# Opening of a two-layer encoder kernel: parameter loads on another queue, weight blocks cut the other way, gate products between q and k, a shift vector summed into columns

## The chip, the cores and the metric

One Trainium2 chip, one of its cores. The metric is device time in microseconds (us) of one launch. TensorE is called PE below, VectorE DVE, ScalarE ACT, GpSimd POOL and SyncE SP, as in the profile. SP computes nothing here: it issues the weight transfers, one after the other.

## The reference

A trunk of two layers on 256 tokens of width 1024. What matters here of each layer:

```
mod = silu(c) @ w_ada[l] + b_ada[l]                  # 6 vectors of 1024
shift1, scale1, gate1, shift2, scale2, gate2 = split(mod, 6)
h = rms_norm(x, norm1_g) * (1 + scale1) + shift1
mq, mk, mv, mo, mgates, aq, ak, av, gm, ga = split(h @ w_in + b_in)
y_m = mlstm_mixer(mq, mk, mv, mo, mgates, conv_w, ...)   # q, k: convolution over 5 tokens, silu
y_a = bidirectional_gqa(aq, ak, av, ...)                 # 8 heads, 2 key heads, rotary
merged = sigmoid(gm) * (y_m @ w_branch_m) + sigmoid(ga) * (y_a @ w_branch_a)
x = x + gate1 * (merged @ w_out)
h2 = rms_norm(x, norm2_g) * (1 + scale2) + shift2
x = x + gate2 * hierarchical_moe(h2, ...)                # 32 experts, 2 a token, 6 MB of weights each
```

All weights are float32 and are read from memory once. `w_ada` is 25 MB a layer, `w_in` 20 MB, the experts 201 MB.

## The kernel before

Each layer has a mixer (`mixer`) and an expert stage (`experts`).

**Weights** come in transfers of 1 MB into a ring of slots: an arena of 16 slots in SBUF, of which four (0, 1, 2, 15) are always ring slots, and three tiles `B`. Other arena slots join when their contents are dead (`release`, the word `free` in `MIX`) and leave again (`withhold`, the word `hold`: the three tiles go). `plan` is the list of all transfers in order. `pump` issues the next ones as long as a slot that suits is free, and `done` gives a slot back. SP keeps the order of the list, so a transfer that waits for its slot holds up all behind it. Each queue's DMAs take eight semaphores in turn, so that one issue also waits for the landing of the one eight before it.

**Products of the mixer.** `h` lies as channels by tokens, 8 blocks of 128 channels, split into a high and a low part (`hh`, `hl`) of the type that PE multiplies fast; each weight block is split in the same way. A *step* is half of the channels (four blocks, `kh`) against 256 columns of `w_in`: 24 matmuls of 128x256. Its preparation (`prep`) is a cast on ACT (128x1024) and two subtractions (`low`), one on DVE and one on POOL, into one of two buffers `R`. A layer has 38 such steps, in the order of `ORDER`: q, k, akv, aq, v, o, gm, ga (`keys`). A transfer of `w_in` holds all channels of 256 columns and so serves two steps. A finished pair of q or k goes through `fin_qk`: per 128 columns a copy on ACT, one `tensor_scalar` and four `scalar_tensor_tensor` on DVE (the convolution), a silu on ACT. A pair of gm or ga is copied by ACT alone (`fin_g`).

**MIX** is a string per layer, written by hand, which interleaves the steps (numbers) with all other work: the mLSTM's gates (`gates`, `gates2`) and its decay vectors (`dec0` to `dec4`; `dec1` is 12 narrow matmuls that need `lf` from DVE), its heads (`ms`, `mo`), attention (`kr`, `qr`, `as`, `at`, `ao`), and the products with `w_ada` (`r4` to `r11` of this layer, `c0` to `c3` of the next). PE and SP keep the order of the program; a scheduler orders ACT, DVE and POOL.

**Products with `w_ada`.** A block of 512 columns takes two transfers and eight matmuls (`ada_part`, 16 rows of the trace), which leave sums in four rows. ACT and DVE split them, two matmuls with a matrix of ones add them up over the rows (`ada_sum`, rows named `prow`), and the result is either turned into columns (`ada_col`: multiply by the identity and reduce) or added to a vector that is the same in all partitions (`ada_row`).

**Opening of layer 0** (`setup`, then the first part of `mixer`): SP issues two blocks of `w_ada` (4 MB), then all small parameters (`params`, 12 DMAs), then two more blocks, then `w_in`. PE takes block 0, then 1, then the transposed `x` (`pxt`), then 2 and 3; shift1 is in blocks 0 and 1, scale1 in 2 and 3. When all 16 columns of `c1` are there, `hh` and `hl` are made, and the steps begin.

**After the steps**, `dense(4)` runs the first four of eight merge products, then 16 matmuls of one row (`psh`, `psj`) turn shift2 (`sh2b`, a row vector in SBUF) into two sets of columns, for the router (`shT`) and for the experts (`sh2c`). The rest of the merges, the product with `w_out`, the router and the experts follow.

Of the kernel before, what the change touches and what calls it, by code (L numbers as in the profile page):

```python
# [18 lines left out]
P = 128  # L19
# [24 lines left out]
ORDER = (("q", 2), ("k", 2), ("akv", 1), ("aq", 2), ("v", 2), ("o", 2), ("gm", 4), ("ga", 4))  # L44
# [3 lines left out]
    "1 gates 3 gates2 dec0 tables 3 dec1 1 c0 dec2 2 dec3 r5 1 dec4 2 kr 1 qr:0 r11 1 kt 2 qr:1 1 r7 1 hold qt:0 1 ms:0 1 c1 qt:1 2 ms:1 1 as:0 r8 mo:0 mo:1 2 r9 ms:3 1 ms:2 at:0 at:4 r4 as:1 mo:2 1 r10 1 at:1 mo:3 ao:0 at:5 r6 1 ao:2 as:2 mn c2 free:7:13:14 2 mt at:2 1 as:3 2 at:3 c3 at:6 at:7 ao:1 1 ao:3 2",  # L48
    "1 tables 1 gates 2 gates2 dec0 3 dec1 1 dec2 2 dec3 1 dec4 1 kr 2 kt r10 1 qr:0 2 qr:1 r6 1 hold 3 ms:0 qt:1 2 r8 ms:1 1 qt:0 mo:0 as:0 1 r9 mo:1 as:1 1 ms:2 r11 at:0 at:4 ms:3 mo:2 2 at:5 1 at:1 mo:3 ao:0 r7 ao:2 1 as:2 mn free:7:13:14 2 at:2 at:6 1 mt as:3 2 at:3 at:7 ao:1 1 ao:3 2")
# [4 lines left out]
def trunk(ctx, tc, x, c, w_ada, b_ada, norm1_g, w_in, b_in, conv_w, conv_b, mlstm_norm_g, q_norm_g, k_norm_g,  # L54
# [135 lines left out]

    keys = [(nm, j) for nm, n in ORDER for j in range(n)]

# [3 lines left out]
    def stream(l):  # L196

        n = sent = 0
        for w in MIX[l].split():
            if w.isdigit():  # L200
                n += int(w)
            elif is_ada(w) and (w[0] != "c" or l + 1 < depth):
                m = min((n + 1) // 2 + 1, len(keys))
                yield from keys[sent:m]
                sent = max(sent, m)
                yield "c" if w[0] == "c" else "r", int(w[1:])
        yield from keys[sent:]

    g1b, gt2b = at(3, 0, D), at(3, D, D)
    A2b, sh2b = at(4, 0, D), at(4, D, D)  # L210
# [11 lines left out]
    def late_loads2(l):  # L222
        for t, o in ((g1b, 2), (sh2b, 3), (A2b, 4), (gt2b, 5))[l > 0:]:
# [4 lines left out]
    def first_params():  # L228
        first["p"] = params(0, nc.sync)

    for l in range(depth):
        if l == 0:
            for b in range(2):
                plan_ada(0, b)
            add(("params", 0), first_params, None)
            for b in range(2, 4):
                plan_ada(0, b)
        else:
            plan_ada(l, EARLY[0])
        for it in stream(l):  # L240
            if it[0] in DENSE:
                o = DENSE[it[0]] + 256 * it[1]
                add((it[0], l, it[1]), w_in[l].rearrange("(k p) c -> p k c", p=P)[:, :, o:o + 256], (8, 256))
# [13 lines left out]
        for j in range(4):  # L257
            add(("wo", l, j), w_out[l].rearrange("(k p) c -> p k c", p=P)[:, :, 256 * j:256 * j + 256], (8, 256))
# [35 lines left out]
    def params(l, q):  # L294
# [23 lines left out]
        p["gqk"] = gqk  # L318
        return p
# [8 lines left out]
    def setup():  # L328
# [3 lines left out]
        pump()  # L332
        V.memset(condp, 0.0)
# [56 lines left out]
    def ada_part(l, b):  # L390
        pb = ps.tile([P, 512], F32, tag="f", name="pada")
        for h in range(2):
# [4 lines left out]
            done("ada", l, b, h)  # L397
        ph, pw = parts_at[0][:, 0, :], parts_at[0][:, 1, :]
# [10 lines left out]
    def ada_col(l, b, parts):  # L409
# [3 lines left out]
        n = 4 if l == 0 else 2  # L413
        dg = at(5, 0, n, P) if l == 0 else at(8, 1556, n, P)
# [5 lines left out]
    def ada_row(l, b, parts):  # L420
# [3 lines left out]
        dst = {2: g1b, 3: sh2b, 4: A2b, 5: gt2b}[kind][:, hs]  # L424
# [7 lines left out]
    def mixer(l, p):  # L432
# [3 lines left out]
        parts_at[:] = [pool.tile([P, 2, 512], F32R, name="part")]  # L436
        st["phase"] = 4 * l
# [14 lines left out]
        def prep():  # L452
# [65 lines left out]
        def fin_qk(j, pq):  # L518
            pre = rot("pre", 5, 0, 2, S + 4)
# [939 lines left out]
```

## Time and profile before

| | us |
|---|---|
| median of three runs | 1512.65 |
| their range | 1510.78 to 1512.72 |
| the profiled execution | 1509.83 |
| its span, first to last instruction | 1508.0 |

PE is busy for 1357.6 us, 90% of the span, DVE for 650.1 us, ACT for 396.5 us, POOL for 266.5 us. 519.77 MB are read. The span falls into four stages: mixer 0 to about 312 us, experts 0 to about 770 us, mixer 1 to about 1036 us, experts 1 to the end. In the page's 40 slices the transfers move about 420 GB/s in both expert stages and between 204 and 346 GB/s in the mixers. A busy share says which engine to look at; what ends a wait is read from the rows of the stage. Idle time of an engine stands in brackets behind the instruction that came after it, with what ended it.

### The profile page before, as it was taken

To read this page: it belongs to the slowest core of one execution; us is meant where nothing else is said; L and a number is where in the kernel's file an instruction comes from. 1 tells how busy PE (TensorE), PEld (TensorE's weight loads), DVE (VectorE), ACT (ScalarE), POOL (GpSimd) and SP (SyncE) were. 2 spreads that over 40 slices of the span, in tenths; PEclk is the share of its full clock that TensorE was granted. 3 is DMA by queue.
4 is the path that set the end of the run, shared out by engine and by line. 5 is a ranking of instruction groups with operands and counts; after the bars stand their busy time and mean duration, and the time that the engine had idled before them with its cause. 6 is when DMAs were issued, how large, how long until landed. Compare 5 with 4: busy or idle time off the path is not lost. (4 is left out here: it accounts for less than half of the span.)

```text
span 1508.0 us, 20315 instructions
## 1 busy us (share of the span) xinstructions
PE 1357.6 (90%) x7878; PEld 794.2 (53%) x7879; DVE 650.1 (43%) x1404; ACT 396.5 (26%) x729; POOL 266.5 (18%) x306
## 2 busy tenths in 40 slices
PE   5799999969999989879978999997999999888996
PEld 1678779934434434334338888994434443334432
DVE  2697774633232322223258867554223323213223
ACT  1444664421111111011035366633111111101101
POOL 1545334500000000000015543560000000000000
PEclk8889999989999999999989999998999999999998
DMA  8967697769999999999996666766999999999995
GB/s 293 338 204 257 226 346 270 273 268 420 422 421 421 420 421 422 421 419 376 418 375 227 217 216 238 241 251 231 421 422 420 421 421 420 421 421 419 376 421 216
DMA packets 146698, 522.24 MB, mean 346 GB/s; under 512 B 15660, under 2 KB 62962, under 8 KB 98466
## 3 DMA queue, kind: packets, MB, share of 16 engines
q1 hardware_dynamic: 140898, 517.20, 87.4%
q10 hardware_dynamic: 4880, 1.87, 0.5%
q0 software_dynamic: 816, 1.78, 0.5%
q8 instruction: 65, 1.06, 0.3%
q14 instruction: 39, 0.32, 0.1%
HBM read 519.77 MB, written 1.05 MB: 345 GB/s over the span
## 5 line engine op out<-in xcount | busy, mean ns | idle before, releaser
L1213 PE MATMUL pgu<-arena 128*64 128x512 f32 x1456 | 349.7, 594 | 20.2 <-DMA arena<-in_w_up_dram 11.7
L1213 PEld LDWEIGHTS pgu<-arena 128*64 128x64 f32 x1456 | 115.1, 137 | 223.5 <-issue 172.7
L1222 DVE SCALAR_TENSOR_TENSOR arena<-pgu,wsl,arena 128x512 f32<-128x512 f32 x32 | 36.4, 1137 | 383.4 <-PE pgu L1213 383.4
L1238 PE MATMUL pd<-arena 128*64 128x512 f32 x720 | 177.7, 594 | 7.3 <-ACT arena L1229 7.3
L441 POOL TENSOR_TENSOR R<-arena,R 128x512 fp32r<-128x512 f32 (+1 forms) x86 | 125.9, 1466 | 168.3 <-ACT R L459 109.9
L1169 POOL TENSOR_TENSOR arena<-oh,arena 128x256 f32<-128x256 f32 x32 | 19.5, 615 | 741.6 <-DVE oh L1163 470.0
L494 PE MATMUL pd<-R,R 128*128 128x256 f32 x1008 | 136.9, 294 | 8.2 <-ACT R L641 5.1
L509 PE MATMUL pd<-R,R 128*128 128x256 f32 x1056 | 134.9, 285 | 4.8 <-DVE R L441 4.8
L494 PEld LDWEIGHTS pd<-R,R 128*128 128x128 f32 x1008 | 129.4, 199 | 18.0 <-issue 6.9
L509 PEld LDWEIGHTS pd<-R,R 128*128 128x128 f32 x1056 | 128.8, 191 | 10.4 <-DVE R L441 5.4
L1249 DVE TENSOR_TENSOR y<-pd,arena 128x512 f32<-128x512 f32 x64 | 44.1, 691 | 202.7 <-PE pd L1238 167.3
L1213 PE MATMUL pgu<-B,arena 128*64 128x512 f32 x432 | 118.1, 594 | 2.7 <-DMA B<-in_w_up_dram 2.7
L441 DVE TENSOR_TENSOR R<-arena,R 128x512 fp32r<-128x512 f32 (+1 forms) x102 | 83.8, 827 | 58.8 <-ACT R L459 51.6
L1238 PEld LDWEIGHTS pd<-arena 128*64 128x64 f32 x720 | 55.2, 137 | 95.3 <-issue 85.6
L1250 ACT CAST yh<-y 128x512 fp32r<-128x512 f32 x64 | 39.6, 619 | 240.4 <-DVE y L1249 240.4
L459 ACT CAST R<-arena 128x1024 fp32r<-128x1024 f32 x78 | 81.2, 1047 | 76.7 <-PE pd L509 26.9
L1185 PE MATMUL pG<-oh,X 128*128 128x256 f32 x512 | 74.3, 309 | 14.4 <-DVE oh L1163 9.2
L1261 DVE TENSOR_TENSOR xs<-xs,psc 128x512 f32<-128x512 f32 x128 | 79.3, 679 | 17.4 <-PE psc L1258 17.4
L1185 PEld LDWEIGHTS pG<-oh,X 128*128 128x128 f32 x512 | 70.9, 216 | 25.2 <-issue 25.2
L1229 ACT COPY arena<-pat 128x512 f32<-128x512 f32 x32 | 18.7, 586 | 220.2 <-PE pat L1228 220.2
L1213 PEld LDWEIGHTS pgu<-B,arena 128*64 128x64 f32 x432 | 37.2, 137 | 74.3 <-issue 63.4
L1189 ACT ACTIVATE arena<-pG,sh2c 128x256 f32<-128x256 f32 x64 | 30.3, 473 | 160.2 <-DVE arena L1191 160.2
(320 smaller groups left out, 1682.7 us busy)
## 6 DMA issues: line engine op xcount, KB each, us to landing
arena<-in_w_up_dram SPq DMA_DIRECT2D x104, 1024.0 KB, 19.8
arena<-in_w_down_dram SPq DMA_DIRECT2D x90, 1024.0 KB, 19.8
arena<-in_w_gate_dram SPq DMA_DIRECT2D x78, 1024.0 KB, 19.8
arena<-in_w_ada_dram SPq DMA_DIRECT2D x36, 1024.0 KB, 9.5
B<-in_w_gate_dram SPq DMA_DIRECT2D x30, 1024.0 KB, 19.8
arena<-in_w_in_dram SPq DMA_DIRECT2D x28, 1024.0 KB, 8.7
B<-in_w_up_dram SPq DMA_DIRECT2D x24, 1024.0 KB, 19.8
X<-in_w_gate_dram SPq DMA_DIRECT2D x20, 1024.0 KB, 19.8
```

The lines of the kernel that those rows point to most:

```text
L441: eng.tensor_tensor(dst, full, hi.bitcast(F32), op=ALU.subtract)
L459: A.copy(wh, w)
L494: T.matmul(acc[key][o][:, 0:S], lhsT=w[:, kk, P * o:P * o + P], rhs=x_[:, 4 * kh + kk], start=kh == 0 and i == 0 and kk == 0, stop=kh == 1 ...
L509: T.matmul(acc[key][t][:, 0:256], lhsT=x_[:, 4 * kh + kk, P * t:P * t + P], rhs=w[:, kk], start=kh == 0 and i == 0 and kk == 0, stop=kh == ...
L1185: T.matmul(pG[:, kk, 0:n], lhsT=x_[:, t, k, :], rhs=oh[:, t, :], start=i == 0, stop=i == 3)
L1189: A.activation(xg[k][:, 0:n], pG[:, kk, 0:n], AF.Identity, bias=sh2c[:, k:k + 1])
L1213: T.matmul(pg[CAP * e:CAP * e + CAP, :], lhsT=xg[4 * h + kk][:, P * (i % 2) + CAP * e:P * (i % 2) + CAP * e + CAP], rhs=w[e][:, kk, :], st ...
L1222: V.scalar_tensor_tensor(ac.rearrange("p k q -> p q k"), pu.rearrange("p (q k) -> p q k", k=4), wsl[:, 0:1], sl.rearrange("p (q k) -> p q ...
L1238: T.matmul(pd[n][CAP * e:CAP * e + CAP, :], lhsT=aT[:, 2 * h + kk, CAP * e:CAP * e + CAP], rhs=w[e][:, kk, 512 * n:512 * n + 512], start=h ...
L1249: V.tensor_tensor(y[:, cs], pd, gt2b[:, cs], op=ALU.mult)
L1250: A.copy(yh[:, cs], y[:, cs])
L1261: V.tensor_tensor(xx, xx, pq, op=ALU.add)
```

## The change

- **Parameters.** `first_params` uses POOL's queue and is called in `setup`, before the masks are made. SP's list begins with the four blocks of `w_ada` in the order 0, 2, 1, 3 (`FIRST`). `params` gains a DMA, the eight-column form `b3` of the bias of shift2.
- **Modulations by halves.** Blocks 0 and 2 give shift1 and scale1 of channel blocks 0 to 3. `ada_fast` copies the sums as they are, `ada_put` turns them into columns with four matmuls of two columns, and `build` makes half of `hh` and `hl`. Then the same for blocks 1 and 3. The first four steps of layer 0 run as q0 and q1 with the first half of the channels, then both with the second half.
- **`w_in` and `w_out`** are cut into transfers of half the channels by 512 columns. One transfer serves steps of two neighbouring keys, and two are needed before a pair of columns is done.
- **Order.** Two of gm's four pairs run between q and k. The words of `MIX` move accordingly: `gates` comes after three steps where it came after one, heads and attention elsewhere. The preparation of weights gets a higher priority for the scheduler (`PREP`). The convolution has three buffers of its own.
- **Shift of the second norm.** Blocks 6 and 7 of `w_ada` go through `ada_shift` and `shift_put`: one copy on ACT, eight matmuls of 64x2 and one addition each, straight to columns. `psh` and `psj`, `sh2b` and its bias load go. The router's weights are read a second time in the column order of `sh2c` (`wr2`, on POOL's queue).

```diff
+FIRST = (0, 2, 1, 3)
+PREP = 100
-ORDER = (("q", 2), ("k", 2), ("akv", 1), ("aq", 2), ("v", 2), ("o", 2), ("gm", 4), ("ga", 4))
+ORDER = (("q", 0, 2), ("gm", 0, 2), ("k", 0, 2), ("akv", 0, 1), ("aq", 0, 2), ("v", 0, 2), ("o", 0, 2), ("gm", 2, 4),
+         ("ga", 0, 4))
...
-        for t, o in ((g1b, 2), (sh2b, 3), (A2b, 4), (gt2b, 5))[l > 0:]:
+        for t, o in ((g1b, 2), (A2b, 4), (gt2b, 5))[l > 0:]:
...
     def first_params():
-        first["p"] = params(0, nc.sync)
+        first["p"] = params(0, nc.gpsimd)
...
-                add((it[0], l, it[1]), w_in[l].rearrange("(k p) c -> p k c", p=P)[:, :, o:o + 256], (8, 256))
+                    add((it[0], l, it[1], h), src[:, 4 * h:4 * h + 4, o:o + 512], (4, 512))
...
+    def ada_fast(b):
+        t = rot("fast", 5, 0, 2, 512)
+        A.copy(t, ada_sums(0, b))
+        return t
+
+    def ada_shift(l, b):
+        A.copy(turned_sums, ada_sums(l, b).rearrange("p (q k) -> p k q", k=KD))
+
+    def shift_put(sh2c, b3, b):
+        o = 64 * (b % 2)
+        pc = ps.tile([P, 512], F32, tag="f", name="pshift")
+        for k in range(KD):
+            T.matmul(pc[o:o + 64, 2 * k:2 * k + 2], lhsT=turned_sums[:, k, :], rhs=ones[:, 0:2], start=True, stop=True,
+                     tile_position=(0, o))
+        V.tensor_tensor(sh2c[o:o + 64, :], pc[o:o + 64, 0:2 * KD].rearrange("p (k o) -> p k o", o=2)[:, :, 0],
+                        b3[o:o + 64, :], op=ALU.add)
+
+    def ada_put(c1, cols, b, t):
+        pc = ps.tile([P, 512], F32, tag="f", name="pcol")
+        for j in range(4):
+            T.matmul(pc[:, 2 * j:2 * j + 2], lhsT=t[:, P * j:P * j + P], rhs=ones[:, 0:2], start=True, stop=True)
+        V.tensor_tensor(c1[:, 4 * b:4 * b + 4], pc[:, 0:8].rearrange("p (j o) -> p j o", o=2)[:, :, 0],
+                        cols[:, 80 + 4 * b:84 + 4 * b], op=ALU.add)
...
-            A.copy(wh, w)
-            low(wl[:, 0:2], w[:, 0:2], wh[:, 0:2], V)
-            low(wl[:, 2:4], w[:, 2:4], wh[:, 2:4], G)
+            with tc.high_priority(offset=PREP):
+                ...
...
+        if l == 0:
+            s = [order.popleft() for _ in range(4)]
+            order.extendleft(reversed([s[0], s[2], s[1], s[3]]))
...
+            for b in FIRST[:2]:
+                ada_put(c1, cols, b, fast[b])
+            build(range(4))
+            for b in FIRST[2:]:
+                fast[b] = ada_fast(b)
+            with tc.high_priority():
+                for b in FIRST[2:]:
+                    ada_put(c1, cols, b, fast[b])
+                build(range(4, 8))
+            dense(1)
...
+        nc.gpsimd.dma_start(wr2[:, :, 0:4], w_rg[l].rearrange("(p k) g -> p k g", k=KD))
+        nc.gpsimd.dma_start(wr2[:, :, 4:36], w_re[l].rearrange("(p k) g -> p k g", k=KD))
...
         dense(4)
-        ph = ps.tile([P, 512], F32, tag="c", name="psh")
-        for k in range(KD):
-            T.matmul(ph[:, 2 * k:2 * k + 2], lhsT=sh2b[0:1, P * k:P * k + P], rhs=ones[0:1, 0:2], start=True, stop=True)
...
-        pj = ps.tile([P, 512], F32, tag="c", name="psj")
-        for k in range(KD):
-            T.matmul(pj[:, 2 * k:2 * k + 2], lhsT=sh2b[0:1, :].rearrange("o (q k) -> o k q", k=KD)[:, k, :],
-                     rhs=ones[0:1, 0:2], start=True, stop=True)
...
         dense(1)
```

On SP, at the start of the program, the transfers stood like this before (`rows` to `gqk` are the parameters, `B` and `arena` the slots):

```order
L167 DMA arena<-in_w_ada_dram 128x4x512 x4
L297 DMA rows<-in_norm_g_dram 8x128
L298 DMA rows<-in_b_in_dram 8x128
L299 DMA rows<-in_b_in_dram 16x128
L300 DMA rows<-in_conv_w_dram 40x128
L301 DMA rows<-in_conv_b_dram 8x128
L302 DMA rows<-in_b_ada_dram 16x128
...
L317 DMA gqk<-in_k_norm_g_dram 128x64
L167 DMA B_87<-in_w_ada_dram 128x4x512
L167 DMA B_88<-in_w_ada_dram 128x4x512
L167 DMA B_89<-in_w_ada_dram 128x4x512
L167 DMA arena<-in_w_ada_dram 128x4x512
L167 DMA arena<-in_w_in_dram 128x8x256 x3
```

Now:

```order
L170 DMA arena<-in_w_ada_dram 128x4x512 x4
L170 DMA B_87<-in_w_ada_dram 128x4x512
L170 DMA B_88<-in_w_ada_dram 128x4x512
L170 DMA B_89<-in_w_ada_dram 128x4x512
L170 DMA arena<-in_w_ada_dram 128x4x512
L170 DMA arena<-in_w_in_dram 128x4x512 x4
L170 DMA B_87<-in_w_in_dram 128x4x512
```

The twelve small loads between the fourth and the fifth transfer are gone from this queue.

On DVE, in mixer 0, around the decay vector `lf` (`R` is prepared weight, L524 and L526 the convolution, `gt` the gates), before:

```order
L672 TENSOR_TENSOR gt<-pg_498,gb 128x32
L441 TENSOR_TENSOR R_158<-arena,R_158 128x512
L524 TENSOR_SCALAR arena<-arena,cols 128x256 x2
L526 SCALAR_TENSOR_TENSOR arena<-arena,cols 128x256 x8
L684 SCALAR_TENSOR_TENSOR ab<-gt 128x16
L441 TENSOR_TENSOR R_157<-arena,R_157 128x512
L524 TENSOR_SCALAR arena<-arena,cols 128x256
L687 SCALAR_TENSOR_TENSOR lf<-gt,ab 128x16
L526 SCALAR_TENSOR_TENSOR arena<-arena,cols 128x256
L524 TENSOR_SCALAR arena<-arena,cols 128x256
L526 SCALAR_TENSOR_TENSOR arena<-arena,cols 128x256 x6
```

Now (L494 prepares weight, L584 and L586 are the convolution):

```order
L586 SCALAR_TENSOR_TENSOR conv<-conv,cols 128x256 x8
L746 TENSOR_TENSOR gt<-pg_502,gb 128x32
L494 TENSOR_TENSOR R_160<-arena,R_160 128x512
L758 SCALAR_TENSOR_TENSOR ab<-gt 128x16
L584 TENSOR_SCALAR conv<-conv,cols 128x256 x2
L586 SCALAR_TENSOR_TENSOR conv<-conv,cols 128x256 x6
L494 TENSOR_TENSOR R_159<-arena,R_159 128x512
L586 SCALAR_TENSOR_TENSOR conv<-conv,cols 128x256 x2
L761 SCALAR_TENSOR_TENSOR lf<-gt,ab 128x16
L494 TENSOR_TENSOR R_160<-arena,R_160 128x512
L772 COPY Bc<-pb 128x16
L494 TENSOR_TENSOR R_159<-B_87,R_159 128x512
```

Ahead of `ab` one pair of columns is convolved instead of two, and the subtraction of a weight cuts into the second pair.

On PE, after the fourth merge product of a mixer (`pm`), before:

```order
L482 MATMUL pm<-Y_1827,R_158 128x256
L482 MATMUL pm<-Y_1826,R_158 128x256
L1009 MATMUL psh<-onesr,arena 128x2 x8
L1014 MATMUL psj<-onesr,arena 128x2 x8
L482 MATMUL pm<-Y_1826,R_157 128x256
```

Now the merges follow on each other there, and the columns are made far ahead, between two steps, twice in a mixer:

```order
L568 MATMUL pd<-R_160,R_157 128x256 x8
L442 MATMUL pshift<-onesr,arena 64x2 x8
L416 MATMUL pada<-arena,condp 32x512 x4
L416 MATMUL pada<-B_87,condp 32x512 x4
L568 MATMUL pd<-R_159,R_157 128x256 x8
```

The 16 matmuls of one row became twice 8 of 64 columns.

## Rows read from the trace of the kernel before

**Rows 1.** Busy time by engine in chosen stretches, granted clock, DMA share, GB/s.

```profile
16.00:24.00 8.00, 8.00 (x50) 4.70 (x50) 2.07 (x3) 0.58 (x1) 0.00 (x0) 1.00 0.42 95
24.00:40.00 16.00, 10.18 (x39) 2.05 (x37) 4.29 (x8) 1.17 (x2) 3.39 (x7) 0.68 1.06 371
40.00:72.00 32.00, 25.87 (x196) 23.27 (x196) 23.65 (x41) 13.55 (x22) 20.30 (x35) 0.84 1.06 358
72.00:84.00 12.00, 8.17 (x40) 7.96 (x41) 9.09 (x20) 8.53 (x13) 3.53 (x8) 0.63 0.13 43
84.00:312.00 228.00, 211.09 (x1656) 182.33 (x1654) 160.99 (x401) 115.62 (x220) 95.24 (x80) 0.96 0.80 275
784.00:1036.00 252.00, 230.46 (x1821) 207.84 (x1821) 176.84 (x433) 132.61 (x247) 114.97 (x112) 0.96 0.69 240
330.00:700.00 370.00, 341.26 (x1645) 143.41 (x1642) 103.22 (x174) 42.94 (x77) 7.95 (x13) 0.99 1.00 416
```

**Rows 2.** Timeline, opening: start, us, engine, line, what, xcount, [idle <-ended by].

```profile
3.50 4.56 SPq L297 DMA_DIRECT2D rows<-in_norm_g_dram  x1
17.56 0.15 PEld L395 LDWEIGHTS pada<-arena,condp 128*32 128x32 f32 x4 [1.10 <-DMA arena<-in_w_ada_dram]
...
36.13 0.33 PEld L395 LDWEIGHTS pada<-arena,condp 128*32 128x32 f32 x8 [1.38 <-DMA arena<-in_w_ada_dram]
...
44.24 0.58 PE L494 MATMUL pd<-R,R 128*128 128x256 f32 x1 [4.36 <-ACT R L641]
...
51.27 1.93 PE L661 MATMUL pg<-R,wg 128*32 128x256 f32 x30
...
54.16 8.90 PE L494 MATMUL pd<-R,R 128*128 128x256 f32 x72
```

**Rows 3.** The cast of a step's weights, from the page's groups (busy, mean ns).

```profile
L459 ACT CAST R<-arena 128x1024 fp32r<-128x1024 f32 x78 | 81.2, 1047 | 76.7 <-PE pd L509 26.9
```

**Rows 4.** Timeline of PE around `dec1` (L692) in mixer 0, and of DVE.

```profile
73.66 1.21 PE L494 MATMUL pd<-R,R 128*128 128x256 f32 x8 [2.02 <-DVE R L441]
77.05 0.59 PE L692 MATMUL pb<-lf,trif 128*128 128x4 f32 x2 [2.17 <-DVE lf L687]
...
79.63 5.47 PE L494 MATMUL pd<-R,R 128*128 128x256 f32 x24
...
91.36 3.02 PE L509 MATMUL pd<-R,R 128*128 128x256 f32 x24
...
76.82 0.17 DVE L687 SCALAR_TENSOR_TENSOR lf<-gt,ab 128x16 f32<-128x16 f32 x1 [1.05 <-ACT ab L686]
```

**Rows 5.** Timeline of PE around `dec1` in mixer 1.

```profile
814.61 0.39 PE L692 MATMUL pb<-lf,trif 128*128 128x4 f32 x2 [2.18 <-DVE lf L687]
...
816.17 3.48 PE L494 MATMUL pd<-R,R 128*128 128x256 f32 x16
```

**Rows 6.** Timeline of PE around the columns of shift2 in mixer 0.

```profile
230.43 0.63 PE L406 MATMUL prow<-part,onesr 128*128 128x512 f32 x2
...
249.40 1.94 PE L1009 MATMUL psh<-onesr,arena 1*128 1x2 f32 x16
251.20 3.94 PE L1014 MATMUL psj<-onesr,arena 1*128 1x2 f32 x16
255.07 5.02 PE L482 MATMUL pm<-Y,R 128*128 128x256 f32 x24
259.93 3.04 PE L482 MATMUL pm<-Y,Y 128*128 128x256 f32 x24
...
268.56 1.87 PE L1026 MATMUL pL<-arena,shT 128*128 128x36 f32 x16
```

**Rows 7.** Landing of ring transfers issued in 140 to 205 us; two products with `w_ada` there.

```profile
DMA to landing us min/median/max: 5.2/7.9/11.0
...
157.25 1.92 PE L395 MATMUL pada<-arena,condp 128*32 128x512 f32 x16
168.22 1.92 PE L395 MATMUL pada<-arena,condp 128*32 128x512 f32 x16
```

More of the change, by code (lines that the diff above doesn't have):

```diff
@@ L189, in plan_ada @@
             add(("ada", l, b, h), s, (4, 512))
-    keys = [(nm, j) for nm, n in ORDER for j in range(n)]
+    keys = [(nm, j) for nm, a, b in ORDER for j in range(a, b)]
+    first_use, s0 = [], 0
+    for nm, j in keys:
+        if nm == "akv":
+            first_use.append(((nm, j), s0))
+        elif j % 2 == 0:
+            first_use += [((nm, j // 2, h), s0 + h) for h in range(2)]
+        s0 += 2
     def is_ada(w):
@@ L202, in stream @@
             elif is_ada(w) and (w[0] != "c" or l + 1 < depth):
-                m = min((n + 1) // 2 + 1, len(keys))
-                yield from keys[sent:m]
-                sent = max(sent, m)
+                while sent < len(first_use) and first_use[sent][1] <= n + 2:
+                    yield first_use[sent][0]
+                    sent += 1
                 yield "c" if w[0] == "c" else "r", int(w[1:])
-        yield from keys[sent:]
+        for it, _ in first_use[sent:]:
+            yield it
     g1b, gt2b = at(3, 0, D), at(3, D, D)
-    A2b, sh2b = at(4, 0, D), at(4, D, D)
+    A2b = at(4, 0, D)
+    turned_sums, wr2 = at(4, D, KD, 64), at(4, D + 512, KD, 36)
     bb = at(6, 0, 1808)
@@ L228, in first_params @@
     def first_params():
-        first["p"] = params(0, nc.sync)
+        first["p"] = params(0, nc.gpsimd)
     for l in range(depth):
         if l == 0:
[L233 to L236, printed above, removed]
+            for b in FIRST:
                 plan_ada(0, b)
@@ L256, in trunk @@
                 add((nm, l, j), w[l].rearrange("(k p) c -> p k c", p=P)[:, :, 512 * j:512 * j + 512], (4, 512))
[L257 to L258 removed]
+        for j in range(2):
+            for h in range(2):
+                add(("wo", l, j, h), w_out[l].rearrange("(k p) c -> p k c", p=P)
+                    [:, 4 * h:4 * h + 4, 512 * j:512 * j + 512], (4, 512))
         for i in range(NPAIR):
@@ L458, in prep @@
             wh, wl = wide(t, 0, 4), wide(t, 1024, 4)
-            A.copy(wh, w)
-            low(wl[:, 0:2], w[:, 0:2], wh[:, 0:2], V)
-            low(wl[:, 2:4], w[:, 2:4], wh[:, 2:4], G)
+            with tc.high_priority(offset=PREP):
+                A.copy(wh, w)
+                low(wl[:, 0:2], w[:, 0:2], wh[:, 0:2], V)
+                low(wl[:, 2:4], w[:, 2:4], wh[:, 2:4], G)
             if last:
@@ L953, in mixer @@
             if w.isdigit():
-                for _ in range(int(w) - (l > 0 and i == 0)):
+                for _ in range(int(w) - (i == 0)):
                     step()
```

97 lines of the change are left out of this document (58 added, 39 removed).

## The prediction, written before the changed kernel ran

> **What bounds the kernel now.** I read the table of stretches first [rows 1]. From 330 to 700 us the transfers run at 1.00 of their engines and 416 GB/s, and PE, busy for 341 of 370 us, waits for them: the expert stages are bound by bytes, which the change leaves as they are. In 84 to 312 us and 784 to 1036 us PE is busy for 211 of 228 and 230 of 252 us, with the transfers at 0.80 and 0.69 and DVE at 70%: the mixers are bound by PE. A microsecond taken from a mixer, or from what stands ahead of it, starts an expert stage that much earlier, and that stage takes as long as before. So each stretch is costed by what ends PE's waits in it.
>
> Then the opening, by the timeline [rows 2]. The first four transfers of `w_ada` (blocks 0 and 1) were there at 17.56 us, when PE's wait for the last of them ended. The other four were there at 36.13. PE's first product with `w_in` began at 44.24, after 4.36 us of waiting for `h` from ACT. From 54.16 us it ran three steps without a break. In 16 to 24 us the transfers ran at 95 GB/s, where the 16 us that followed had 371 [rows 1]: SP stood in the list of small loads (the first held it for 4.56 us [rows 2]), each behind the landing of a transfer eight places earlier. So the opening waits for bytes, and eight microseconds of them were mostly not asked for.
>
> Last, two places inside the mixers. Around `dec1` PE waits 2.02 us for a prepared weight, 2.17 us for `lf`, which stands on DVE behind two pairs of convolutions, and then goes on at half the clock: a step takes 5.47 us there and 3.02 later [rows 4]. The granted clock in 72 to 84 us was 0.63 [rows 1], between the two levels of 1.2 and 2.4 GHz. Around `psh` and `psj` PE is busy all the time, but with 32 rows of hardly any work, and at half clock from `psj` on [rows 6].
>
> **The opening: -10.5.** Four transfers of 1.049 MB at 371 GB/s take 2.83 us each. Asked for at once, the last four land at 17.56 + 4 x 2.83 = 28.9 us instead of 36.13. From the hole alone: (1 - 95/371) x 8 = 6.0 us gained; the two bounds are 6.0 and 7.2. The first transfer of `w_in` stands next in the queue: 28.9 + 2.83 = 31.7. Half of `h` is made by then, since blocks 0 and 2 are the first to land, so the first step waits only for its own weight: a cast of 1.05 us [rows 3] after 31.7, with two or three copies and activations of ACT mixed in, 32.8 to 34. The small loads now fall among these transfers, and the router's second set with its short runs too. No row has their price beside large transfers; the bounds are nothing and 2.5 us, half of the 5.2 us that the fastest transfer took from issue to landing [rows 7]. I take 34.5 for the first step, range 33 to 36.5.
>
> From there the same work is compared, three steps and the gates. After: one step at half clock 5.47, 1.2 more until the clock is up, two steps at 3.02 [rows 4], gates 1.93 [rows 2]: 34.5 + 14.6 = 49.1. Before: at 54.16 one step and the gates were done, and two more took two thirds of 8.90 [rows 2]: 60.1. Gain 11.0, of which I leave half a microsecond to POOL: its DMA issues now stand ahead of the masks, and the subtractions for `h` behind layer 1's first loads. Both are hidden while the first step is later than 33 us; without that cover POOL's issues would push it. Bounds -8 and -13.
>
> On such moves the Trainium skill (Trainium Kernel Development and Optimization, Key Constraints) says that queues of different engines run on the same 16 DMA engines, so that issuing from several saves only issue time. By it the parameters' move is worth at most the hole, 6 us. I take more in total, because the second part (half of `h` early, less after the last landing) is no matter of queues.
>
> **Convolutions apart, `dec1`: -5.5 and -3.** In mixer 0 the loss is 2.02 + 2.17 + (5.47 - 3.02) = 6.6 us, and about 1 in the narrow matmuls of `dec1` at half clock [rows 4]: 7.6. In mixer 1 the rows show 2.18 and, for 16 of 24 matmuls, 3.48 - 2.01 = 1.47, together 3.65 [rows 5]. Now the steps behind q are gm's, which ask nothing of DVE but half a subtraction, and weights are prepared between convolutions. Before `lf` there is still one pair of convolutions and a part of the second, and on ACT the silu of the first pair waits ahead of the second pair's copies, two table loads and a cast. Counted from the end of step three, `lf` comes after some 13 to 15 us, PE is there after 14.4 (gates 1.93, four steps, a little for `gates2`). So 0 to 2.5 us of waiting remain: -5.5 in mixer 0 (0 to -7.6) and -3 in mixer 1 (0 to -3.7). The k columns are now convolved beside akv and the decay vectors. I take that as even, +-2.
>
> **Shift into columns: -5.1 in each mixer.** Gone are 1.94 + 3.94 - 0.2 of overlap = 5.7 us, and the half clock behind them, 5.02 - 3.04 = 2.0: 7.7 [rows 6]. New are twice 16 rows of `pshift`. Nearest is the product of 36 columns, 1.87 us for 16 rows [rows 6]; less two `prow` pairs of 0.63, which go, that is 2 x (1.87 - 0.63) = 2.5. After those 1.87 us no clock was lost, which is why I count none here. If each `pshift` did cost the half clock, 2.0 us each, the gain is 1.2. Bounds -1 and -6.5. ACT's strided copy takes the place of a cast of the same size, and DVE loses a subtraction of 512 columns: nothing. The bias vector of shift2 was 0.5 MB a layer that now needn't be moved; it lay beside PE's work.
>
> **Slots: +1.** A transfer of `w_in` now stays until its second use, three steps instead of two, and both halves must be there for a pair. After `hold` there are four slots. Before, a gate pair held one of them, now two, and the products with `w_ada` have to take turns in the other two. For r9, r10 and r6 the second half is asked for when the first half of the block before has been used, and PE comes to it 6.5 to 8 us later by the order of `MIX` (one step 3.0, one head 1.4 to 1.8, the product itself 1.92 and its sum). Landing took 5.2 to 11.0 us there, 7.9 in the middle, when three or four transfers were under way [rows 7]; with two it is nearer the low end. I take +1, bounds 0 and +6.
>
> **Sum.** -10.5 - 5.5 - 3 - 5.1 - 5.1 + 1 = -28.2. The profiled execution took 1509.83 us, so 1481.6; its kernel's median is 1512.65, 2.8 higher, and the forecast for the median is **1484 us**. With all bounds on the good side: -13 - 7.6 - 3.7 - 6.5 - 6.5 - 2 = -39, 1473. On the bad side: -8 - 0 - 0 - 1 - 1 + 6 + 2 = -2.
>
> **The rivals.** *Less of each (1501).* The opening stays a matter of bytes and gives the hole's 6.0, `lf` is late again, since ACT's chain of silu, copies and table loads only changed places, and `pshift` loses the clock: -6 - 1 - 1 - 1.2 - 1.2 = -10.4, with the slots' +1 -9.4 and a median near 1503; a little better with half of `dec1`, 1501. For it: the same resources do the same work, and before `lf` ACT has the same pieces. Against it: the order shows `ab` behind one pair less.
>
> *Slots become the bound (1522).* The queue of ring transfers keeps its order, so one that waits for a slot holds those behind it. If landings in the four-slot stretch take 12 us or more instead of 7.9, six products with `w_ada` there wait: r9 and r10 5.5 each, r6 4, the rest 1 to 2, some 18 us; every wait of more than 2 us was followed by a step at half clock, 2.45 more [rows 4, 5], five times, 12; and mixer 1 has four such blocks, another 10. That is 40 against the gain of 29: 1512.65 + 10. The point from which it decides is a landing of about 11 us. For it: PE came to these products every 11 us before [rows 7] and now every 7 in places. Against it: the stretch has 0.80 of the transfer engines at most on average, and fewer transfers under way land sooner.
>
> *The change doesn't do what it says (1512).* That would be if the small loads of POOL came so late that the transposed parameters held up PE behind `pxt`. PE reaches them near 23 us, and POOL begins at about 1 us.
>
> *Bytes early on.* The Trainium skill (DMA: Bandwidth & Descriptors, Specifications) wants runs of at least 512 bytes for full rate. The router's second read has runs of 16 and 128 bytes and stands in the opening. No row here shows what it takes beside large ones; by the bound of 2.5 us above it is inside the range.
>
> **Chances.** The forecast with its own range (1473 to 1496) 0.68, less of each 0.17, the change without effect 0.05, slots the bound 0.08, better than 1473 0.02. The range for 8 in 10 takes in the first and most of the second: 1472 to 1504. A measurement of this kernel can tell about 0.2%, 3 us, from no change. Faster by more: 0.87; within: 0.05; slower: 0.08.
>
> **What would show it.** In the changed trace: transfers near 370 GB/s from 4 to 40 us without a hole; the eighth transfer of `w_ada` used near 30 us, the first step at 34.5, three steps and gates done near 49. No wait above 1 us before `dec1`, steps of 3.0 behind it. `pshift` near 1.9 us and the step behind it at 3.0; merges without a break and 7.7 us shorter. PE's waits before products with `w_ada` on a transfer: none above 2 us. Mixer 0 ends near 290 us (312 before), mixer 1 lasts 8 us less, and the expert stages keep their length to 1 us. If one of these lengths changes, or PE waits for landings in the four-slot stretch, the prediction is wrong in its frame, not in a size.

## The result, and the profile of the changed kernel

The changed kernel is slower: its median is 1523.27 us against 1511.94 for the kernel before in the same runs, a ratio of 1.0070 with a 95% interval of 1.0053 to 1.0087. The forecast was 1484, with a range of 1472 to 1504. The profiled execution has a span of 1522.0 us, 14.0 more than before. Its page begins:

```profile
span 1522.0 us, 20289 instructions
PE 1353.5 (89%) x7894; PEld 791.9 (52%) x7895; DVE 627.6 (41%) x1388; ACT 398.0 (26%) x731; POOL 285.3 (19%) x324
```

PE and DVE have less to do than before and the kernel takes longer, so the difference is waiting. Five landmarks of PE divide the two traces: the first product with `w_in`, the first product after the router (`pp`) of each layer, and the first transposed `x` (`pxt`) of layer 1.

| stretch | before, us | after, us | difference |
|---|---|---|---|
| start to first step | 44.24 | 40.29 | -3.95 |
| mixer 0: first step to `pp` | 266.09 | 270.19 | +4.10 |
| router and experts 0: `pp` to `pxt` | 470.23 | 469.21 | -1.02 |
| mixer 1: `pxt` to `pp` | 253.43 | 270.17 | +16.74 |
| router and experts 1: `pp` to the end | 474.01 | 472.14 | -1.87 |

The sum is 14.0. The first step comes 3.95 us earlier where 9.7 were forecast (44.24 - 34.5), and both mixers, which should have become shorter, became longer. These are the two mixers, before and after (columns as in [rows 1]):

```profile
44.24:310.33 266.09, 244.82 (x1887) 213.36 (x1887) 188.17 (x447) 135.10 (x252) 116.49 (x119) 0.94 0.80 272
780.56:1033.99 253.43, 233.36 (x1830) 210.82 (x1831) 177.06 (x429) 133.18 (x248) 114.75 (x111) 0.96 0.70 240
```

```profile
40.29:310.48 270.19, 240.62 (x1883) 208.20 (x1883) 175.83 (x436) 133.24 (x248) 122.93 (x117) 0.95 0.76 268
779.69:1049.86 270.17, 240.50 (x1826) 213.41 (x1827) 173.46 (x425) 136.26 (x251) 118.28 (x110) 0.91 0.63 226
```

In mixer 1 PE was idle for 253.43 - 233.36 = 20.1 us before and for 29.7 now, and it is busy for 7.1 us longer with about the same instructions, at a granted clock of 0.91 instead of 0.96. In mixer 0 idle time rose from 21.3 to 29.6, and less busy time made up for half of it.

What PE waits for in mixer 1 is in the list of its waits (line, what it waited for, us in total, times, longest). Its two longest entries, the waits of `pxt` and `pp` at the two ends of the stretch, come to 13.5 us before and 12.2 after and are left out here. The next ones before:

```profile
PE prow L406 <- DVE part L400: 2.2, 1, 2.2
PE pb L692 <- DVE lf L687: 2.2, 1, 2.2
PE pd L509 <- DVE R L441: 1.6, 1, 1.6
```

And after:

```profile
PE pb L766 <- DVE lf L761: 4.2, 1, 4.2
PE pkt L860 <- DVE arena L835: 3.8, 2, 2.3
...
PE po L986 <- DVE arena L976: 3.2, 1, 3.2
...
PE ppt L974 <- DVE arena L966: 2.1, 2, 1.9
PE pn L899 <- DVE arena L880: 2.0, 1, 2.0
```

The waits for prepared weights are nearly gone. In their place PE waits for `lf`, for the rotated keys (`pkt`), for attention (`po`, `ppt`) and for a head (`pn`). In mixer 0 the two longest new waits look like this in the timeline of PE. Each row names what came last before PE went on; the first will need POOL's timeline to be understood.

```profile
55.81 8.15 PE L553 MATMUL pd<-R,R 128*128 128x256 f32 x66
68.20 1.65 PE L553 MATMUL pd<-R,R 128*128 128x256 f32 x6 [4.23 <-POOL conv L581]
69.64 0.42 PE L766 MATMUL pb<-lf,trif 128*128 128x4 f32 x2
...
175.66 0.77 PE L899 MATMUL pn<-arena 128*128 128x129 f32 x2 [5.38 <-DVE arena L890]
...
178.51 3.04 PE L416 MATMUL pada<-arena,condp 128*32 128x512 f32 x16
```

`pn` belongs to `mo:2`, which stands right behind `ms:2` in the new `MIX`. PE comes from the one to the other with nothing between, while ACT and DVE still work on the head. The sixteen rows of `pada` behind it take 3.04 us, where the same ones took 1.92 [rows 7]. The granted clock was 0.50 in 174.0 to 178.5 us, with that wait in it, and 0.61 in the three us behind: a wait is paid again in clock.

### The profile page after: what moved, and what is told of

It is laid out like the page before. It is cut to its first block, busy times and chain, and to the rows that moved or that the text cites. A ratio compares the mean times of both kernels' runs of the same rounds, so it can differ in the third digit from the quotient of the medians.

```text
span 1522.0 us, 20289 instructions
## 1 busy us (share of the span) xinstructions
PE 1353.5 (89%) x7894; PEld 791.9 (52%) x7895; DVE 627.6 (41%) x1388; ACT 398.0 (26%) x731; POOL 285.3 (19%) x324
## 3 DMA queue, kind: packets, MB, share of 16 engines
q10 hardware_dynamic: 4880, 1.87, 0.5%
## 5 line engine op out<-in xcount | busy, mean ns | idle before, releaser
L494 POOL TENSOR_TENSOR R<-arena,R 128x512 fp32r<-128x512 f32 (+1 forms) x78 | 119.2, 1532 | 145.8 <-ACT R L513 102.4
L553 PE MATMUL pd<-R,R 128*128 128x256 f32 x1008 | 137.6, 297 | 7.6 <-POOL conv L581 4.2
L568 PE MATMUL pd<-R,R 128*128 128x256 f32 x1056 | 138.7, 291 | 5.2 <-DVE arena L609 3.6
L553 PEld LDWEIGHTS pd<-R,R 128*128 128x128 f32 x1008 | 131.1, 203 | 18.0 <-issue 7.9
L568 PEld LDWEIGHTS pd<-R,R 128*128 128x128 f32 x1056 | 132.8, 197 | 12.0 <-DVE arena L609 4.7
L494 DVE TENSOR_TENSOR R<-arena,R 128x512 fp32r<-128x512 f32 (+1 forms) x94 | 83.1, 895 | 71.4 <-ACT R L513 60.5
L513 ACT CAST R<-arena 128x1024 fp32r<-128x1024 f32 x70 | 73.0, 1044 | 63.1 <-PE pd L553 26.2
```

Source lines behind the costliest of these rows:

```text
L494: eng.tensor_tensor(dst, full, hi.bitcast(F32), op=ALU.subtract)
L553: T.matmul(acc[key][o][:, 0:S], lhsT=w[:, kk, P * o:P * o + P], rhs=x_[:, 4 * kh + kk], start=kh == 0 and i == 0 and kk == 0, stop=kh == 1 ...
L568: T.matmul(acc[key][t][:, 0:256], lhsT=x_[:, 4 * kh + kk, P * t:P * t + P], rhs=w[:, kk], start=kh == 0 and i == 0 and kk == 0, stop=kh == ...
```

## The experiments

All times are medians; a ratio is to the kernel before in the same runs. "Mixer 0" and "mixer 1" are the stretches of the table above in each run's trace, one trace a kernel. From round to round the median of the kernel before lay between 1510.8 and 1512.1 us, so a difference of about 1 us between two rows says nothing.

| kernel | first step | mixer 0 | mixer 1 | us | ratio, 95% |
|---|---|---|---|---|---|
| before | 44.24 | 266.1 | 253.4 | 1511.94 | |
| changed | 40.29 | 270.2 | 270.2 | 1523.27 | 1.0070 (1.0053 to 1.0087) |
| old_order | 40.33 | 259.6 | 258.1 | 1503.54 | 0.9949 (0.9932 to 0.9966) |
| no_prep | 39.58 | 269.4 | 256.2 | 1507.83 | 0.9979 (0.9968 to 0.9991) |
| moved_words | 39.47 | 264.2 | 269.9 | 1517.73 | 1.0047 (1.0029 to 1.0065) |
| late_router | 38.09 | 269.2 | 270.3 | 1519.53 | 1.0061 (1.0041 to 1.0081) |
| order_and_prep | 40.20 | 259.8 | 249.4 | 1494.48 | 0.9892 (0.9875 to 0.9908) |
| params_pool | 39.90 | 265.7 | 255.0 | 1507.08 | 0.9969 (0.9957 to 0.9982) |
| best_old | 38.30 | 260.4 | 251.8 | 1494.38 | 0.9887 (0.9870 to 0.9903) |
| best_new | 38.21 | 263.6 | 254.2 | 1500.04 | 0.9922 (0.9905 to 0.9938) |
| shift_back | 39.02 | 273.3 | 257.2 | 1512.47 | 1.0001 (0.9991 to 1.0010) |
| cut_back | 39.89 | 270.9 | 263.2 | 1520.71 | 1.0067 (1.0045 to 1.0088) |
| tables_behind | 40.38 | 261.8 | 270.3 | 1513.11 | 1.0006 (0.9995 to 1.0017) |
| best_tables | 39.59 | 258.5 | 250.5 | 1493.23 | 0.9883 (0.9866 to 0.9899) |
| new_repaired | 39.45 | 256.0 | 252.7 | 1492.45 | 0.9869 (0.9853 to 0.9886) |
| order_by_layer | 38.88 | 257.4 | 249.7 | 1492.35 | 0.9867 (0.9850 to 0.9883) |

**Order or priority?** Two parts of the change could have made the chains late: the order of the program (`ORDER` and `MIX`), and the priority that lets the preparation of weights go first on ACT, DVE and POOL (`PREP`). Each was taken back alone, and then both.

old_order:

```diff
-ORDER = (("q", 0, 2), ("gm", 0, 2), ("k", 0, 2), ("akv", 0, 1), ...
+ORDER = (("q", 0, 2), ("k", 0, 2), ("akv", 0, 1), ..., ("gm", 0, 4), ("ga", 0, 4))
-MIX = ("3 gates 1 gates2 dec0 tables 3 dec1 ...
+MIX = ("1 gates 3 gates2 dec0 tables 3 dec1 ...
```

> The changed kernel with ORDER and MIX of the kernel before (gm's four pairs together, heads and attention where they stood); opening, cut of the transfers, PREP and the columns of the shift as changed. If the waits come from the order (words of MIX put behind their producers with no step between), they go: mixer 1 lasts 255 to 260 us instead of 278, mixer 0 is some 8 us shorter, time 1493 to 1500. If the priority of the weights (PREP) makes the chains late, or if the cut of the transfers does through the slots, the waits stay with the old order: 1515 or more.

no_prep:

```diff
-            with tc.high_priority(offset=PREP):
-                A.copy(wh, w)
-                ...
+            A.copy(wh, w)
+            ...
```

> The changed kernel without the higher priority for the preparation of weights. Theory of the order: the same waits at the same words, 1519 to 1527. Theory of the priority: DVE and ACT come to lf, the heads and attention earlier, 1512 or less. A third way: weights come late, as PE waited for them before the change, and the time rises above 1527.

order_and_prep is both together.

> The changed kernel with ORDER and MIX of before and without the priority of the weights: what is left of the change is the opening, the cut of the transfers and the columns of the shift. If order and priority cost each on its own, their gains add up: 1523.3 - 19.7 - 15.4 = 1488. If they are two ways into the same waits (either alone leaves the chains time enough), it stays near the better of the two: 1499 to 1505.

Neither theory was alone. The order gave back 19.7 us, 10.6 in mixer 0 and 12.1 in mixer 1; the priority 15.4, 14.0 of them in mixer 1. Both together gave 28.8, of 35.1 if they had added up: they are mostly separate costs with some 6 us in common. How the priority costs is to be read at `lf` in mixer 1, on ACT (L759 and L760 make `ab`, from which DVE makes `lf`). In the changed kernel:

```profile
812.59 1.28 ACT L759 ACT_TABLE_LOAD   x1
...
814.36 1.03 ACT L513 CAST R<-arena 128x1024 fp32r<-128x1024 f32 x1
815.41 1.28 ACT L760 ACT_TABLE_LOAD   x1
816.71 0.21 ACT L760 ACTIVATE ab<-ab 128x16 f32<-128x16 f32 x1
```

And without the priority:

```profile
809.90 1.28 ACT L758 ACT_TABLE_LOAD   x1
...
811.79 1.28 ACT L759 ACT_TABLE_LOAD   x1
813.09 0.22 ACT L759 ACTIVATE ab<-ab 128x16 f32<-128x16 f32 x1
...
813.57 1.99 ACT L512 CAST R<-arena 128x1024 fp32r<-128x1024 f32 x2
```

With it, the cast of a weight (1.03 us) goes between the two table loads, and another went ahead of a silu before them; both weights are for steps behind `dec1`, which waits for `lf`. On DVE a subtraction cuts into the convolutions, whose last one ends 7.7 us behind `gt` instead of 5.9. Without it both casts come after `lf` is on its way. PE's wait for `lf` is 4.2 us with and 1.1 without:

```profile
PE po L985 <- DVE arena L975: 2.9, 1, 2.9
...
PE pkt L859 <- DVE arena L834: 1.7, 1, 1.7
...
PE pb L765 <- DVE lf L760: 1.1, 1, 1.1
```

What PE does behind that wait shows the second price, the clock. With the priority the granted clock was 0.50 in 817 to 820 us, behind the wait, and 0.65 over the two steps that follow; without it 1.00 in 813.5 to 815 and 0.77 over the same two steps. The last pair of `dec1` and these two steps, with the priority and without it:

```profile
819.48 0.57 PE L771 MATMUL pb<-lf,trib 128*128 128x4 f32 x2
819.90 8.63 PE L553 MATMUL pd<-R,R 128*128 128x256 f32 x48
```

```profile
814.71 0.36 PE L770 MATMUL pb<-lf,trib 128*128 128x4 f32 x2
814.93 7.48 PE L552 MATMUL pd<-R,R 128*128 128x256 f32 x48
```

**Which words of the order?** moved_words puts `ms:2` and `mo:2` (`ms:3` and `mo:2` in layer 1) a step apart, and `tables` behind `dec1`.

```diff
-... dec0 tables 3 dec1 1 c0 ... ms:3 1 as:0 ms:2 mo:2 r4 1 as:1 ...
+... dec0 3 dec1 tables 1 c0 ... ms:3 ms:2 1 as:0 r4 1 mo:2 as:1 ...
```

> The changed kernel with three local moves in MIX: tables behind dec1 in layer 0 (its 6.7 us on POOL no longer ahead of a weight's subtraction), and in both layers the two heads one after the other with a step between the last and mo:2. Theory of the order: the waits of 4.23, 5.38 and 2.04 us go, with 2 to 4 us of half clock behind them: 1507 to 1514. Rival: what PE waits for is the DVE as a whole, and the next word waits instead: 1519 or more.

It gained 5.5 us, and by the trace from one of its three moves. In mixer 0 the wait of 5.38 us shrank to 0.96 and the mixer lost 6.0 us. In mixer 1 the head's 2.04 went, but PE waited 1.62 at `as:1` instead and the mixer kept its length. And the wait of 4.23 us stood where it was: POOL's order had not changed. `tables` is a word for POOL, and POOL's instructions are ordered by the scheduler, which put the tables into the same gap again. What they do there in the changed kernel is in POOL's timeline (L816 writes a part of the tables, L494 is half of a weight's subtraction):

```profile
59.31 4.28 POOL L816 TENSOR_TENSOR arena<-arena,gqk 128x32 f32<-128x32 f32 x4
...
64.50 0.87 POOL L816 TENSOR_TENSOR arena<-arena,gqk 128x32 f32<-128x32 f32 x4
...
66.87 1.27 POOL L494 TENSOR_TENSOR R<-arena,R 128x512 fp32r<-128x512 f32 x1
```

PE had done 66 of 72 matmuls. In the third step the next one needs POOL's half of the low part, which ended at 68.14; PE went on at 68.20. The row names a memset (`conv`), which merely ended last. In the kernel before, the same word stood ahead of three steps too, and the tables ran from 55.4 us on, mostly ahead of the convolutions; in the changed kernel they came from 58.8 us on, beside convolutions and ahead of this subtraction. tables_behind has the word behind `dec1` in layer 0, as moved_words, and besides holds the tables back by data:

```diff
+            if l == 0:
+                G.tensor_copy(ctab[:, :, 0, 0:2], al[:, 0, :, 0:2])
+                G.tensor_copy(stab[:, :, :, 0:32:16], al[:, :, :, 0:2])
```

> The changed kernel with the rotary tables of layer 0 held back on POOL until al is there (two tiny copies of al into the tables' places ahead of them, which the tables overwrite). moved_words had moved only the word, and POOL's order stayed. If PE's wait of 4.23 us at 64 us is for the weight's subtraction behind the tables on POOL, it goes, with some half clock: 1516 to 1520. If the subtraction is late for another reason, the wait stays: 1522 to 1525.

The wait was gone, and the gain was 10.2 us (9.7 by the ratios), more than expected: mixer 0 became 8.4 us shorter, twice the wait. The four instructions that had taken 4.28 us took 0.90 in their new place:

```profile
65.02 1.59 POOL L494 TENSOR_TENSOR R<-arena,R 128x512 fp32r<-128x512 f32 x1
...
69.24 0.90 POOL L819 TENSOR_TENSOR arena<-arena,gqk 128x32 f32<-128x32 f32 x4
```

**Slots.** The rival named in the prediction came out at 1522, almost the measured time, so it had to be tried: cut_back gives `w_in` its old transfers (the list of first uses goes with them).

```diff
-                    add((it[0], l, it[1], h), src[:, 4 * h:4 * h + 4, o:o + 512], (4, 512))
+                add((it[0], l, it[1]), src[:, :, o:o + 256], (8, 256))
```

> The changed kernel with w_in in transfers of all channels by 256 columns, as before; w_out, order and priority as changed. If the slots are what made it slow (two transfers for a pair, each kept until its second use), the time falls by 10 us or more, to 1513 or less. If the waits come from order and priority, it stays at 1519 to 1527.

The time stayed: 2.6 us less, with intervals that overlap. PE's waits on transfers in the changed mixers are one of 0.4 us, and the long waits stood in cut_back as before it (4.25 for `lf`, 5.39 for the head). So the rival had the time and not the mechanism. The cut is not free in that trace, though: mixer 1 was 7 us shorter with the old cut, and the stretches from `pp` on together 3.5 us longer. One trace does not tell whether that is the cut.

**The opening.** params_pool moves only the parameters, in the kernel before; late_router takes only the router's second read out of the changed opening and puts it at the end of `late_loads2`.

```diff
-            add(("params", 0), first_params, None)
...
-        first["p"] = params(0, nc.sync)
+        first["p"] = params(0, nc.gpsimd)
```

> The kernel before with one part of the change alone: the parameters on POOL's queue, called in setup; SP's list then begins with four blocks of w_ada without a break. By the prediction's hole (95 GB/s for 8 us) the eighth transfer lands 6 to 7 us earlier, 29 to 30 us instead of 36.09, and the time falls to 1505 or 1506. If the small loads take the same transfer time wherever they stand, the fourth lands later than 17.5 us, the eighth at 34 to 35, and the time falls by 2 at most.

```diff
-        nc.gpsimd.dma_start(wr2[:, :, 0:4], w_rg[l].rearrange("(p k) g -> p k g", k=KD))
-        nc.gpsimd.dma_start(wr2[:, :, 4:36], w_re[l].rearrange("(p k) g -> p k g", k=KD))
...
+        nc.sync.dma_start(wr2[:, :, 0:4], ...)
+        nc.sync.dma_start(wr2[:, :, 4:36], ...)
```

> The changed kernel with the second read of the router's weights issued by SP behind the late loads instead of by POOL in the opening. If these reads (1024 runs of 16 and 128 bytes each) take the transfers' time in the opening, the fourth transfer of w_ada lands at 20 to 22 us instead of 24.04, the eighth at 31 to 33 instead of 34.87, and the first step begins 2 to 4 us earlier; time 1519 to 1521. If the parameters themselves take it, landings and time stay: 24, 34.9, 1523.

In params_pool the fourth transfer landed at 21.85 us and the eighth at 32.75, 3.3 earlier than before: between the two expectations. Its time fell by 3.7 us. In late_router they landed at 21.83 and 32.67, against 24.04 and 34.87 in the changed kernel, as expected. But the changed kernel's trace is the latest of the eight that have this read in the opening: their eighth transfers landed at 33.4 to 34.9 us, 34.0 on average, and those of the five with the read late at 32.7 to 33.2, 32.9 on average. So of the 6 to 7 us that were hoped for from the hole, the parameters use about half wherever they stand, and the router's second read takes about one more, not 2.2. The view of the transfers in 0 to 40 us shows the loads of POOL's queue (queue q0: packets, MB, share of 16 engines) before and after:

```profile
q0 software_dynamic: 192, 0.05, 0.6%
```

```profile
q1 hardware_dynamic: 5779, 11.49, 81.7%
...
q0 software_dynamic: 688, 0.41, 9.5%
```

0.41 MB take 9.5% of 40 us, 3.8 us of all transfer engines; a megabyte took three times as much of the engines in these pieces as on SP's queue (23% against 7%).

**The shift.** shift_back is order_and_prep with `psh` and `psj` again (the old lines after `dense(4)`, `sh2b` and its load; no `ada_shift`, `shift_put`, `wr2`).

> order_and_prep with the columns of shift2 made as before (psh and psj after the fourth merge, the row vector and its bias load, no second read of the router's weights). By the traces the merges take 7.5 us less with the change and two pshift of 1.09 stand for two prow of 0.63: 6.6 us a mixer come back, 1494.5 + 13 = 1507 to 1509. By the prediction's term of 5.1 each 1504.7. If the place is hidden by something else, 1495.

The columns are worth 18 us there (16.5 by the ratios), more than any term said. The stretch from the first merge to `pp` is 64.6 to 65.1 us in every kernel that has them and 72.5 before; in shift_back it is 73.3 and 72.0 against 64.6 in order_and_prep, 16.1 us for both layers. Another 4.8 lie ahead of it in mixer 0, where PE of shift_back waits 2.75 us inside a sum (`prow`) at 198 us and order_and_prep has a `pshift` and no wait; what else is in them is not divided here.

**Together.** best_old is order_and_prep with the router's second read late; best_new is the new order with no priority, the moved heads and the late read; best_tables is order_and_prep with the tables held back; new_repaired is best_new with the tables held back; order_by_layer takes new_repaired's order in layer 0 and the old one in layer 1.

> As order_and_prep, and the second read of the router's weights behind SP's late loads as in late_router. If that read costs the opening 2 us wherever it is made alone, 2 to 4 us less than order_and_prep; if the opening is hidden behind dec1's wait for lf, no difference.

> The changed kernel's own ORDER with the three repairs together: no priority for the weights, the words moved as in moved_words, the router's second read late. If the repairs touch different waits: 1523.3 - 15.4 - 5.5 - 3.7 = 1498.7. If they overlap, 1502 to 1507, no better than no_prep.

> order_and_prep with the tables held back in the same way. PE waits 4.73 and 4.00 us for prepared weights around dec1 there. If POOL's tables, and what they push into the convolutions, set the first: 1488 to 1492. If DVE's convolutions set both: 1494.

> best_new (the changed kernel's own order, no priority, heads moved, the router's second read late) with the tables of layer 0 held back as in tables_behind. If gm between q and k does what the prediction wanted in mixer 0 and only the tables undid it, the wait of 4.05 us at 62 us goes and the time falls by 6 to 9 us, to 1491 to 1494, level with the old order. If the order itself is the worse one, the wait comes back elsewhere: 1497 to 1500.

> As new_repaired in layer 0, and the order of before (ORDER and MIX) in layer 1. By the runs so far mixer 1 is 3 to 5 us shorter with the old order, mixer 0 some 4 us shorter with the new one once heads and tables are moved: 1487 to 1490, faster than both pure orders. If the order in mixer 0 gains nothing even so, 1493 to 1495.

In the old order nothing more was to be had: best_old gave none of its 1.9 us at the first step, and best_tables 1.3 us, no more than the noise: PE still waits 3.90 and 4.00 us around `dec1`, for subtractions that stand on DVE behind six convolution instructions each (3.46 and 4.50 us). In the new order the repairs added up for the most part (30.8 us of 34.8): 1507.8 without the priority, 1500.0 with heads and read moved, 1492.5 with the tables held back. So gm between q and k is as fast as the old order with its tables held back, within the intervals; its mixer 0 is the shortest of all with 256.0 us, and from the first step until 109 us no wait of more than 0.9 us is left there. order_by_layer had the shorter mixer 1 as expected (249.7) and gained nothing: the stretches behind the mixers became 5 us longer, 470.8 and 464.6 us up to the last product against 467.8 and 462.3. Why they did stays open. new_repaired and order_by_layer, alike within their intervals, beat both kernels by 1.3 and 2.0%.

## Why the prediction was wrong

**The frame.** That the mixers are bound by PE, the expert stages by bytes, and that a stretch is worth what ends PE's waits in it, held: PE's waits explain the result, and the expert stretches kept their length to 1.9 us (the prediction had said 1). What failed was the list of waits. The prediction priced the waits that the trace of before showed and took two edits as part of a gain or at nothing: the priority ("weights are prepared between convolutions" was its whole working) and the words of `MIX` away from `dec1` (heads, attention and `tables` had no term at all). Taken back one at a time, the priority had cost 15.4 us, and the new order of the words 10.2 through the tables on POOL and 5.5 through a head. Without these three, and with the late read, the kernel runs at 1492.5, inside the range and still 8 us above the forecast; of these the opening explains about 3, the rest is not divided.

**Opening, -10.5: a size.** Three steps and the gates were done at 50.60 + 1.93 = 52.5 us instead of the forecast 49.1 and 60.1 before: -7.6, just outside the bounds. The first 16 us before, then the first 24 after (columns as in [rows 1]), and the way to the first step after:

```profile
0.00:16.00 16.00, 5.05 (x18) 1.02 (x19) 3.92 (x25) 4.39 (x8) 3.82 (x23) 1.00 0.87 323
```

```profile
0.00:16.00 16.00, 3.10 (x16) 0.44 (x17) 1.56 (x10) 3.81 (x7) 13.26 (x43) 1.00 0.88 261
16.00:24.00 8.00, 2.70 (x12) 0.20 (x8) 1.92 (x16) 0.58 (x1) 0.09 (x4) 1.00 1.05 331
```

```profile
34.91 1.06 PE L416 MATMUL pada<-arena,condp 128*32 128x512 f32 x8
35.91 1.95 PE L451 MATMUL pcol<-onesr,arena 128*128 128x2 f32 x16
...
38.28 1.02 ACT L694 ACTIVATE R<-pxt,c1b,A 128x256 fp32r<-128x256 f32 x2 [1.57 <-DVE A L690]
...
39.20 1.04 ACT L513 CAST R<-arena 128x1024 fp32r<-128x1024 f32 x1
...
40.29 10.38 PE L553 MATMUL pd<-R,R 128*128 128x256 f32 x72 [2.44 <-ACT R L513]
...
50.60 1.93 PE L735 MATMUL pg<-R,wg 128*32 128x256 f32 x32
```

The term that failed is the landing. The hole is gone, but in 0 to 16 us the transfers move 261 GB/s where they moved 323, with their engines as busy (0.88 and 0.87). The fourth transfer landed at 24.04 us, where the sum had left it at 17.56. The next four came 2.71 us apart, close to the forecast 2.83, the eighth at 34.87 instead of 28.9 and the first one of `w_in` at 37.69 instead of 31.7. From there to the first step, at 40.29 instead of 34.5, it took 2.6 us, where 2.8 were forecast. The hole had been priced by its GB/s, at 6.0. In the same row [rows 1] the engines' share in it is 0.42: they were busy for 3.4 of the 8 us, so by that row no more than 4.6 could be won, and params_pool won 3.3.

A smaller part is in the order. The first step was to wait for its own weight alone. It stands behind the products of the other two blocks and their columns (`pcol`, until 37.86), and ACT cast its weight only behind two activations for the second half of `h`. ACT was idle when the weight landed, so by these rows the cast could have begun up to 39.20 - 37.69 = 1.5 us earlier (an estimate). The early half of `h` gained nothing here. The forecast of half clock was wrong to the kernel's favour: the sum had 12.7 us for the three steps, with 1.2 "until the clock is up" that no row shows, and they took 10.38 at a granted clock of 0.83 (11.33 at 0.75 in tables_behind).

**`dec1`, -5.5 and -3.** In mixer 0 the mechanism was right: `lf` was made at 63.6 us, 6 us before PE asked for it. The wait that took its place was not on the list. So that the opening's gain is not counted twice, the count runs from the end of the three steps and the gates to the end of the step behind `dec1`, the same work in each kernel. That step in the changed kernel and in tables_behind:

```profile
72.06 4.41 PE L553 MATMUL pd<-R,R 128*128 128x256 f32 x24
```

```profile
66.81 3.10 PE L553 MATMUL pd<-R,R 128*128 128x256 f32 x24
```

It is 85.1 - 60.1 = 25.0 us before, 76.5 - 52.5 = 24.0 in the changed kernel and 69.9 - 53.6 = 16.3 in tables_behind (gates done at 53.56). So the term gave 1.0 where 5.5 were forecast, and 8.7 with the tables held back, above its bound of 7.6. In mixer 1 `lf` was late, as the rival "less of each" had it, but for a reason of its own: PE waited 2.2 us for it before, 4.2 with the priority and 1.1 without.

**Shift, -5.1 each.** Right in mechanism and too small.

```profile
140.38 1.09 PE L442 MATMUL pshift<-onesr,arena 128*64 128x2 f32 x16
141.40 1.07 PE L416 MATMUL pada<-arena,condp 128*32 128x512 f32 x8
```

`pshift` took 1.09 us, not 1.87, and no clock was lost behind it. With 7.47 from the merges and two `prow` of 0.63 [rows 6] saved, that is 7.47 - 2 x (1.09 - 0.63) = 6.6 a mixer by the rows, at the upper bound of 6.5. By shift_back it is 8 to 9 a mixer; the difference is a longer stretch of merges there and the 4.8 us in mixer 0, of which only one wait is named.

**Slots, +1.** The term could not be told from nothing in the time; what the 7 us of mixer 1 in cut_back's trace are stays open. The rival built on the slots is refuted by cut_back, although its 1522 is the nearest number in the prediction to the result: a hit of the number by luck.

## What to carry to other kernels

Price every edit of an order, also those that are meant to change nothing: for each word that moves, write down what PE finds done when it comes there, engine by engine, and give a priority a price on every chain that it overtakes. The busy share of the transfer engines, not GB/s, tells how much of a hole can be free. On an engine that a scheduler orders, a moved word may move nothing, where a dependence on data does. A time that fits a rival is no proof of it.

## What the runs showed of the hardware

POOL and DVE hold each other up on two-input work in SBUF. The tables' four instructions of 128x32 took 0.88 us in the kernel before with DVE at rest, 4.28 beside DVE's convolutions in the changed one, and 0.90 again in tables_behind. The convolutions kept their 0.41 us each. Of the 4.28 a single instruction took 3.28; in each of the six traces with this order and the tables not held back, one of them took 3.27 to 3.47. On POOL before, and on DVE after:

```profile
55.84 0.88 POOL L742 TENSOR_TENSOR arena<-arena,gqk 128x32 f32<-128x32 f32 x4
```

```profile
59.42 2.45 DVE L586 SCALAR_TENSOR_TENSOR conv<-conv,cols 128x256 f32<-128x256 f32 x6
```

In old_order it went the other way. A subtraction of DVE that takes 0.69 us elsewhere took 3.62 while POOL made two of its own (1.31 and 1.28):

```profile
57.30 3.62 DVE L494 TENSOR_TENSOR R<-arena,R 128x512 fp32r<-128x512 f32 x1
```

```profile
57.76 1.31 POOL L494 TENSOR_TENSOR R<-arena,R 128x512 fp32r<-128x512 f32 x1
```

The Trainium skill (SBUF — State Buffer, SBUF: two separate sides) describes a pair of ports that DVE and GpSimd share under an exclusive lock, so that the loser blocks for a whole instruction. The traces agree that one blocks while the other keeps its speed, and show more than that: in the changed kernel POOL's 3.28 us lie beside six convolutions, and in old_order DVE's 3.62 beside two subtractions, so the loser can wait through several instructions of the other engine.
